# Last output columns taken token tile by token tile, three key splits placed ahead of the residual adds, nine constant products in the first gap, spreads as transposes

## The chip, the cores and the metric

The kernel runs on one core of a Trainium2 chip, in one launch. The metric is the device time of that launch in microseconds, the median of several runs. The time before is 1063.87 us, median of 3 runs (1063.2 to 1066.58).

The engines are named as in the profile: PE (TensorE, the products), DVE (VectorE), ACT (ScalarE), POOL (GpSimd), SP (SyncE, which issues most of the DMAs). PEld is the loading of a product's stationary operand.

## The reference, cut to what matters

Two layers of a streaming encoder over 512 tokens of width 1024, with a memory of 256 tokens. All values are 32-bit floats.

```python
for l in range(DEPTH):                       # 2
    h = rms_norm(x, norm_g[l])
    proj = h @ w_in[l]                       # pool, attention, indexer, memory query, gates
    y_pool = multi_scale_pool(...) * silu(pool_z)
    y_attn = dsa_attention(...) * silu(az)   # 8 heads, 128 selected keys a query
    mk, mv = split(rms_norm(mem, mem_norm_g[l]) @ w_mem_kv[l])
    y_mem = memory_attention(mq, mk, mv) * silu(mz)   # 4 heads of 128
    g = sigmoid(gates)                       # three gates a channel
    merged = g0 * (y_pool @ w_branch[l, 0]) + g1 * (y_attn @ w_branch[l, 1]) + g2 * (y_mem @ w_branch[l, 2])
    x = x + merged @ w_out[l]
return rms_norm(x, final_g)
```

`rms_norm(x, g)` is `x * rsqrt(mean(x * x) + EPS) * g` over the 1024 channels of a token.

## The kernel before, in words

**Products in three terms.** Nearly every operand is split into a high part (`whi`, `hh`, `memh`, `mgh`), a cast of it to the type fp32r, and a low part (`wlo`, `hl`, `meml`, `mgl`), the rest; a product is then hi x hi + hi x lo + lo x hi, three matmuls into one PSUM bank (`mm3`, `mm3v`). A weight chunk of 128 x 1024 is fetched by a DMA on SP's queue (`raw_chunk`, L165), cast by ACT (L173, `whi`) and subtracted by DVE, or by POOL where `eng=G` is given (L152 and L177, `wlo`). Raw chunks, `whi` and `wlo` have four buffers each, so a chunk's cast waits until PE has done with the chunk four before.

**Order.** The program's order is that of the source, which a scheduling layer then rearranges among instructions that are free to move; `tc.issue_after` and `behind_pe` pin a block behind a named instruction. Within an engine the order is then fixed. PSUM has eight banks by tag: `pj` 3, `at` 2, `tr` 2, `pv` 1.

**Start (layer 0).** 15 constant products of a 128 x 128 tile of ones, `busy`, run on PE first (L358 to L360). Then the memory's keys: 96 matmuls in four chunks. Then, behind them, `norm_cols` (L235): the squares of x, added up over the eight channel tiles by ACT (L229) and DVE (L232), are summed over the channels by products with a column of `ones`; `rstd_cols` turns the sums into the inverse root with a multiply-add on DVE (L215) and a power on POOL (L216). `spread` (L219) makes a 128 x 512 bank from the four columns of the result, each by a product of the column, broadcast to 128 x 128, with the identity. The memory's values stand in four groups of 12 matmuls (`mem_v`) between these steps: group, spread, group, the memory's column sums (of squares that POOL adds up, L417), group, the memory's spread, group. `norm_x` (L243) makes hf, hh and hl from x and the spread on DVE and ACT, and the index projection (`w_idx`, 24 matmuls into `tr`) reads them.

**Layer.** Projections, the indexer's scores, the selection in rounds on DVE, attention heads and branch projections follow. Then the output projection `out_half` (L311) for the two halves f of the output columns: for each of four chunks c of `w_out`, for each of four token tiles t, six matmuls into the tile's bank; after all of them four adds to the residual (L323, DVE), four squares with a sum (L324, ACT) and, in layer 0, the store of x for the next layer (L326, ACT's queue).

**Between the layers** (L938 to L964). The next layer's memory keys, four groups of 24 matmuls of 256 columns (`mem_k`), stand on PE after the output projection. The first and the second group's low parts were written for DVE and two others for POOL (`eng=G`), the latter behind the norm's power; the scheduling layer has moved groups so that the chunks are fetched in the order 0, 2, 3, 1, chunks 0 and 1 are split on DVE and chunks 2 and 3 on POOL, and PE runs chunk 0, then 2 and 1 interleaved, then 3. `rstd_of` (L329) makes the tokens' inverse root, `xr` the scaled x (L948 ACT, L949 DVE), `turn_x` (L336) turns it into `hh` and `hl` by PE transposes (L341), two channel tiles at a time, between the key groups and the first value groups.

**End (layer 1).** Half 0 is multiplied by the final gain on POOL (L933). After half 1, for each token tile: inverse root, `finish` (L346): two products by it on ACT and DVE (`o`) and a store each on ACT's and SP's queue.

## Time and profile before

| | us |
|---|---|
| median of 3 runs | 1063.87 |
| the profiled execution, its own time | 1065.19 |
| its span, first to last instruction | 1063.0 |
| what lies around the span | 2.19 |
| PE busy in the span | 1047.3 |
| DVE, ACT, POOL busy | 698.0, 474.1, 219.9 |
| mean granted clock of PE | 0.992 |

A row of a timeline has start, length, engine, source line, operation, out<-in, shapes and, in brackets, how long the engine had been idle before it and what ended that. A row of a list of waits has the waiting engine and line, what it waited for, total us, times and the longest. A row of a windows table has the stretch, its length, each engine's busy time with the number of instructions, then the granted clock, DMA share and GB/s; the tables below that were asked for PE alone have one busy column. A 32-bit product with a 128 x 128 moving operand that is not a transpose appears as two records. PE's lengths overlap, since products are pipelined, so their starts are compared.

### The profile page before, as it was taken

To read this page: it belongs to the slowest core of one execution; us is meant where nothing else is said; L and a number is where in the kernel's file an instruction comes from. 1 tells how busy PE (TensorE), PEld (TensorE's weight loads), DVE (VectorE), ACT (ScalarE), POOL (GpSimd) and SP (SyncE) were. 2 spreads that over 40 slices of the span, in tenths; PEclk is the share of its full clock that TensorE was granted. 3 is DMA by queue.
4 is the path that set the end of the run, shared out by engine and by line. 5 is a ranking of instruction groups with operands and counts; after the bars stand their busy time and mean duration, and the time that the engine had idled before them with its cause. 6 is when DMAs were issued, how large, how long until landed. Compare 5 with 4: busy or idle time off the path is not lost.

```text
span 1063.0 us, 13609 instructions
## 1 busy us (share of the span) xinstructions
PE 1047.3 (99%) x5024; PEld 883.4 (83%) x5024; DVE 698.0 (66%) x1273; ACT 474.1 (45%) x860; POOL 219.9 (21%) x293
## 2 busy tenths in 40 slices
PE   8999999999999999999999999999999999999996
PEld 8888888888888888888888888888888888888885
DVE  6757878787788855543374588787768887444342
ACT  7555554322555543432354545533236564333332
POOL 2301440002134410121060133100113333002131
PEclk9999999999999999999999999999999999999998
DMA  8432226323322322435354222222333331233332
GB/s 302 141 120 74 80 74 185 98 72 122 117 95 75 100 80 80 139 100 178 119 170 134 84 80 73 77 81 78 129 100 109 99 101 60 80 99 99 102 117 79
DMA packets 37986, 114.23 MB, mean 107 GB/s; under 512 B 4248, under 2 KB 6296, under 8 KB 37920
## 3 DMA queue, kind: packets, MB, share of 16 engines
q1 hardware_dynamic: 36048, 110.20, 31.5%
q10 hardware_dynamic: 1872, 3.17, 0.8%
q8 instruction: 39, 0.64, 0.2%
q14 instruction: 27, 0.22, 0.1%
HBM read 109.14 MB, written 6.84 MB: 109 GB/s over the span
## 4 chain that ended last, share of the span: by engine, by line
PE 92%; issue 4%; DMA 1%; ACT 1%; DVE 1%; POOL 0%; SPq 0%; ACTq 0%; POOLq 0%
PE pj L87 72%; PE at L87 8%; PE pv L87 6%; PE tr L87 2%; PE tr L607 2%; DMA wraw<-in_w_mk 1%; DMA x<-in_xT 1%; POOL sg L748 0%; DVE wlo L177 0%; ACT o L348 0%; ACT whi L173 0%; SPq L258 0%; PE at L341 0%; PE tr L341 0%; DVE sg L744 0%
## 5 line engine op out<-in xcount | busy, mean ns | idle before, releaser
L173 ACT CAST whi<-wraw 128x1024 fp32r<-128x1024 f32 (+1 forms) x174 | 182.0, 1046 | 375.1 <-PE pj L87 218.3
L87 PE MATMUL pj<-hh,whi 128*128 128x512 f32 (+1 forms) x848 | 330.2, 389 | 0.0
L87 PE MATMUL pj<-hh,wlo 128*128 128x512 f32 (+1 forms) x848 | 328.4, 387 | 0.0
L87 PE MATMUL pj<-hl,whi 128*128 128x512 f32 (+1 forms) x848 | 328.4, 387 | 0.0
L152 DVE TENSOR_TENSOR wlo<-wraw,whi 128x1024 fp32r<-128x1024 f32 x156 | 198.0, 1270 | 156.7 <-ACT whi L173 156.2
L87 PEld LDWEIGHTS pj<-hh,wlo 128*128 128x128 f32 x848 | 159.2, 188 | 32.1
L87 PEld LDWEIGHTS pj<-hl,whi 128*128 128x128 f32 x848 | 159.3, 188 | 30.6
L87 PEld LDWEIGHTS pj<-hh,whi 128*128 128x128 f32 x848 | 159.3, 188 | 30.6
L748 POOL TENSOR_TENSOR sg<-sg,sg 128x512 f32<-128x512 f32 x32 | 52.0, 1624 | 238.4 <-DVE sg L744 238.4
L87 PE MATMUL pj<-yh,whi 128*128 128x512 f32 x192 | 75.1, 391 | 0.0
L87 PE MATMUL pj<-yh,wlo 128*128 128x512 f32 x192 | 74.7, 389 | 0.0
L87 PE MATMUL pj<-yl,whi 128*128 128x512 f32 x192 | 74.7, 389 | 0.0
L792 POOL TENSOR_TENSOR p<-rel,acc 128x256 f32<-128x256 f32 (+2 forms) x48 | 61.3, 1298 | 0.5
L792 POOL TENSOR_TENSOR p<-rel,mask 128x128 f32<-128x128 f32 x16 | 7.4, 463 | 253.6 <-DMA rel<-bias_row 248.7
L744 DVE SCALAR_TENSOR_TENSOR sg<-sg,pj 128x512 f32<-128x512 f32 x48 | 32.9, 685 | 36.0 <-PE pj L87 35.9
L580 DVE MATCH_REPLACE8 acc<-m,acc 128x256 f32<-128x256 f32 (+2 forms) x96 | 51.4, 543 | 0.0
L579 DVE MAX8 m<-acc 128x8 f32<-128x256 f32 (+2 forms) x96 | 49.0, 548 | 0.1
L808 DVE CUSTOM_DVE_ANT_0 p<-at,p 128x128 f32<-128x128 f32 (+1 forms) x64 | 29.9, 490 | 27.6 <-PE at L87 23.8
L87 PEld LDWEIGHTS pj<-yh,wlo 128*128 128x128 f32 x192 | 36.0, 188 | 7.6
L87 PEld LDWEIGHTS pj<-yl,whi 128*128 128x128 f32 x192 | 36.1, 188 | 7.2
L87 PEld LDWEIGHTS pj<-yh,whi 128*128 128x128 f32 x192 | 36.0, 188 | 7.2
L813 DVE TENSOR_SCALAR p<-p,ast 128x128 f32<-128x128 f32 (+1 forms) x64 | 41.5, 678 | 0.3
(240 smaller groups left out, 1714.9 us busy)
## 6 DMA issues: line engine op xcount, KB each, us to landing
wraw<-in_w_tiled SPq DMA_DIRECT2D x112, 512.0 KB, 3.4
wraw<-in_w_br SPq DMA_DIRECT2D x24, 512.0 KB, 3.5
wraw<-in_w_out SPq DMA_DIRECT2D x16, 512.0 KB, 3.5
wraw<-in_w_mv SPq DMA_DIRECT2D x8, 512.0 KB, 4.6
wraw<-in_w_av SPq DMA_DIRECT2D x8, 512.0 KB, 3.8
rel<-bias_row SPq DMA_DIRECT2D x16, 256.0 KB, 3.8
wraw<-in_w_mk SPq DMA_DIRECT2D x7, 512.0 KB, 4.4
bias_row<-bias_one SPq DMA_DIRECT2D x8, 320.0 KB, 6.9
```

What stands on the lines that cost most here:

```text
L87: on_pe[:] = [T.matmul(*a, **kw)]
L152: eng.tensor_sub(out_lo, src, hi)
L173: A.copy(hi[:, :n], raw[:, :n])
L579: V.max(m8, a[:, :n])
L580: V.match_replace(out=a[:, :n], in_to_replace=m8, in_values=a[:, :n], imm_value=TAKEN)
L607: T.transpose(pt[:, i * P:(i + 1) * P], col_of(qb, kb), ident)
L744: last = V.scalar_tensor_tensor(s, s, 1.0, ps, op0=ALU.add, op1=ALU.mult)
L748: G.tensor_add(acc[j], acc[j], s)
L792: G.tensor_add(probs[h][:, Q_COL[qb]:Q_COL[qb] + n], rels[h][:, 512 - n:512], mb[:, :n])
L808: V.tensor_tensor_reduce(out=pq, in0=ps[:, :n], in1=pq, op0=ALU.add, op1=ALU.min, scale=-1.0, scalar=3e38, accum_out=st[:, 0, qb:qb + 1])
L813: V.tensor_scalar(pq, pq, st[:, 2, qb:qb + 1], None, op0=ALU.mult)
```

## The change

Five edits. The spread's products become transposes of the same broadcast columns (L223 after). Nine constant products are put between the memory's keys and the norm's column sums of layer 0. `out_half` becomes `out_part`, `out_add` and `out_banks`; half 0 of the last layer and both halves of layer 0 keep their order. In the last layer half 1 has its four chunks split first, and then each token tile runs through all four chunks, is added, squared, scaled and stored before the next. In layer 0 the next layer's first two key chunks are fetched and split between the last product of half 1 and its adds, the third behind the first key group, the fourth behind the second, all on DVE; and the transposes take their places after the third and fourth key group and after the first two value groups.

```diff
@@ -96,6 +96,7 @@
 
     N_S2 = 49
     N_BUSY = 15
+    N_GAP = 9
     SH1, PUMP1, PUMP2 = 0, 2, 9
     IQ_AT = (2, 3)
     MS = (2, 4, 5)
@@ -219,8 +220,7 @@
 
         pb = bank(tag)
         for b in range(nb):
-            matmul(pb[:, b * P:(b + 1) * P], r[:, b:b + 1].to_broadcast([P, P]), ident,
-                     start=True, stop=True)
+            on_pe[:] = [T.transpose(pb[:, b * P:(b + 1) * P], r[:, b:b + 1].to_broadcast([P, P]), ident)]
         return pb
 
     def norm_add(sums, k, xk, n=S, apart=KT - 1):
@@ -308,22 +308,24 @@
         return mv
 
 
-    def out_half(l, f, x, ssq):
-
-        bks = [bank("pv"), pj(), pj(), pj()] if f == 0 else [bank("at"), bank("at"), bank("tr"), bank("tr")]
-        for c in range(4):
-            hi, lo = chunk(w_out[l, f, c])
-            for t in range(NQ):
-                for a in range(2):
-                    k = 2 * c + a
-                    w = slice(a * 512, a * 512 + 512)
-                    tk = slice(t * P, t * P + P)
-                    mm3v(bks[t], mg_hi[k][:, tk], mg_lo[k][:, tk], hi[:, w], lo[:, w], k == 0, k == KT - 1)
-        for t in range(NQ):
-            V.tensor_add(x[t][f], x[t][f], bks[t])
-            A.activation(s2("sq"), x[t][f], AF.Square, scale=1.0 / 32, accum_out=ssq[:, f, t:t + 1])
-            if l + 1 < DEPTH:
-                nc.scalar.dma_start(x1[t * P:(t + 1) * P, f * 512:(f + 1) * 512], x[t][f])
+    def out_part(t, c, part, ps):
+
+        hi, lo = part
+        for a in range(2):
+            k = 2 * c + a
+            w = slice(a * 512, a * 512 + 512)
+            tk = slice(t * P, t * P + P)
+            mm3v(ps, mg_hi[k][:, tk], mg_lo[k][:, tk], hi[:, w], lo[:, w], k == 0, k == KT - 1)
+
+    def out_add(l, f, t, x, ssq, ps):
+
+        V.tensor_add(x[t][f], x[t][f], ps)
+        A.activation(s2("sq"), x[t][f], AF.Square, scale=1.0 / 32, accum_out=ssq[:, f, t:t + 1])
+        if l + 1 < DEPTH:
+            nc.scalar.dma_start(x1[t * P:(t + 1) * P, f * 512:(f + 1) * 512], x[t][f])
+
+    def out_banks(f):
+        return [bank("pv"), pj(), pj(), pj()] if f == 0 else [bank("at"), bank("at"), bank("tr"), bank("tr")]
 
     def rstd_of(ssq, ts):
 
@@ -405,6 +407,10 @@
                 matmul(o, w[:, c], r[k], start=k == 0 and h % 2 == 0 and n == 0, stop=k == KT - 1 and n == 2,
                        skip_group_check=True)
     with behind_pe():
+        ps = bank("at")
+        for i in range(N_GAP):
+            matmul(ps[:, :P], busy, busy, start=True, stop=True)
+    with behind_pe():
         r = norm_cols(sums)
     with tc.issue_after(on_dve[0].ins):
         parts_v[2:] = [split_chunk(raw, eng=V) for raw in parts_v[2:]]
@@ -926,40 +932,51 @@
             grow = s2("grow"), s2("grow")
             for f in range(2):
                 nc.sync.dma_start(grow[f], g_row[:, f * 512:(f + 1) * 512].to_broadcast([P, 512]))
-        for f in range(2):
-            out_half(l, f, x, ssq)
-            if last and f == 0:
+        for f in range(1 if last else 2):
+            bks = out_banks(f)
+            for c in range(4):
+                part = chunk(w_out[l, f, c])
                 for t in range(NQ):
+                    out_part(t, c, part, bks[t])
+            if f == 1:
+                ck = [chunk(w_mk[l + 1, h], eng=V) for h in range(2)]
+            for t in range(NQ):
+                out_add(l, f, t, x, ssq, bks[t])
+                if last:
                     G.tensor_mul(x[t][0], x[t][0], grow[0])
         if last:
+            parts_o = [chunk(w_out[l, 1, c]) for c in range(4)]
+            bks = out_banks(1)
             for t in range(NQ):
-                r = rstd_of(ssq, slice(t, t + 1))
-                finish(t, x, r, grow)
+                for c in range(4):
+                    out_part(t, c, parts_o[c], bks[t])
+                out_add(l, 1, t, x, ssq, bks[t])
+                finish(t, x, rstd_of(ssq, slice(t, t + 1)), grow)
         else:
             banks = []
-            mem_k(l + 1, 0, mh, ml, chunk(w_mk[l + 1, 0], eng=V), banks)
+            mem_k(l + 1, 0, mh, ml, ck[0], banks)
+            ck.append(chunk(w_mk[l + 1, 2], eng=V))
             r = rstd_of(ssq, slice(0, NQ))
-            with tc.issue_after(on_pool[0].ins):
-                c2, c3 = (chunk(w_mk[l + 1, h], eng=G) for h in (2, 3))
-            mem_k(l + 1, 1, mh, ml, chunk(w_mk[l + 1, 1], eng=V), banks)
+            mem_k(l + 1, 1, mh, ml, ck[1], banks)
+            ck.append(chunk(w_mk[l + 1, 3], eng=V))
+            mem_k(l + 1, 2, mh, ml, ck[2], banks)
             xr = []
             for t in range(NQ):
                 xr.append([s2("xr"), s2("xr")])
                 A.mul(xr[t][0], x[t][0], r[:, t:t + 1])
                 V.tensor_scalar(xr[t][1], x[t][1], r[:, t:t + 1], None, op0=ALU.mult)
             turn_x(l + 1, xr, (0, 4))
-            mem_k(l + 1, 2, mh, ml, c2, banks)
+            mem_k(l + 1, 3, mh, ml, ck[3], banks)
             turn_x(l + 1, xr, (1, 5))
-            mem_k(l + 1, 3, mh, ml, c3, banks)
-            turn_x(l + 1, xr, (2, 6))
             mkf = mem_k_norm(banks)
             pv = [pj(), bank("pv")]
             for c in range(4):
                 part = chunk(w_mv[l + 1, c], eng=G)
                 for b in range(2):
                     mem_v(l + 1, c, b, mh, ml, part, pv)
-                if c == 0:
-                    turn_x(l + 1, xr, (3, 7))
+                if c < 2:
+                    turn_x(l + 1, xr, (2 + c, 6 + c))
+                if c == 1:
                     mk = mem_k_end(mkf)
             mv = mem_v_end(pv)
```

The three places at which the instructions stand otherwise, as rows of one engine in program order. PE in layer 0, from the last matmul of the memory's keys (`pj` from `memh` and `wlo`) to the first value group; before:

```order
L87 MATMUL pj_309<-memh_244,wlo_240 128x256
L87 MATMUL tr_408<-ones,sq_278 128x1 x4
L87 MATMUL tr_408<-ones,sq_298 128x1 x4
L87 MATMUL pj_310<-whi_300,memh_196 128x512
L87 MATMUL pv_311<-whi_300,memh_196 128x512
```

After:

```order
L87 MATMUL pj_309<-memh_244,wlo_240 128x256
L87 MATMUL at_408<-busy 128x128 x9
L87 MATMUL tr_418<-ones,sq_278 128x1 x4
L87 MATMUL tr_418<-ones,sq_298 128x1 x4
L87 MATMUL pj_310<-whi_300,memh_196 128x512
L87 MATMUL pv_311<-whi_300,memh_196 128x512
```

A row of nine products of `busy` stands between the keys and the column sums.

DVE between the layers, from the split of the last `w_out` chunk on: `wlo` rows are splits of weight chunks, `x` rows the residual adds, `rs_v` the norm, `xr` the scaled x; before:

```order
L152 TENSOR_TENSOR wlo_4742<-wraw_4739,whi_4741 128x1024
L177 TENSOR_TENSOR wlo_4788<-wraw_4785,whi_4787 128x1024
L323 TENSOR_TENSOR x_4489<-x_4489,at_4645 128x512
L323 TENSOR_TENSOR x_4491<-x_4491,at_4646 128x512
L323 TENSOR_TENSOR x_4493<-x_4493,tr_4647 128x512
L323 TENSOR_TENSOR x_4495<-x_4495,tr_4648 128x512
L332 SCALAR_TENSOR_TENSOR rs_v_4816<-ssq_4504 128x4
L949 TENSOR_SCALAR xr_4863<-x_4489,rs_r_4817 128x512
L177 TENSOR_TENSOR wlo_4835<-wraw_4832,whi_4834 128x1024
L949 TENSOR_SCALAR xr_4867<-x_4491,rs_r_4817 128x512
L949 TENSOR_SCALAR xr_4871<-x_4493,rs_r_4817 128x512
L949 TENSOR_SCALAR xr_4875<-x_4495,rs_r_4817 128x512
```

After:

```order
L153 TENSOR_TENSOR wlo_4752<-wraw_4749,whi_4751 128x1024
L178 TENSOR_TENSOR wlo_4782<-wraw_4779,whi_4781 128x1024
L178 TENSOR_TENSOR wlo_4788<-wraw_4785,whi_4787 128x1024
L178 TENSOR_TENSOR wlo_4835<-wraw_4832,whi_4834 128x1024
L322 TENSOR_TENSOR x_4499<-x_4499,at_4655 128x512
L322 TENSOR_TENSOR x_4501<-x_4501,at_4656 128x512
L322 TENSOR_TENSOR x_4503<-x_4503,tr_4657 128x512
L322 TENSOR_TENSOR x_4505<-x_4505,tr_4658 128x512
L334 SCALAR_TENSOR_TENSOR rs_v_4838<-ssq_4514 128x4
L967 TENSOR_SCALAR xr_4898<-x_4499,rs_r_4839 128x512
L178 TENSOR_TENSOR wlo_4869<-wraw_4866,whi_4868 128x1024
L967 TENSOR_SCALAR xr_4902<-x_4501,rs_r_4839 128x512
```

Two more splits, of the second and third key chunk, stand ahead of the four adds; the row behind the first `xr` is the split of the key chunk that is fetched last (`w_mk` 1 before, 3 after). On POOL the two splits that stood right behind the norm's power are gone, and the first value chunk's split stands there.

ACT in the last layer, from the square of half 1's first token tile on: `sq` are squares, `o` the products by the inverse root, DMA the stores; before:

```order
L324 ACTIVATE sq_9220,ssq_8950<-x_8935 128x512
L324 ACTIVATE sq_9223,ssq_8950<-x_8937 128x512
L324 ACTIVATE sq_9226,ssq_8950<-x_8939 128x512
L324 ACTIVATE sq_9229,ssq_8950<-x_8941 128x512
L348 ACTIVATE o_9235<-x_8934,rs_r_9232 128x512
L348 ACTIVATE o_9245<-x_8936,rs_r_9242 128x512
L350 DMA out<-o_9235 128x512
L350 DMA out<-o_9245 128x512
L348 ACTIVATE o_9255<-x_8938,rs_r_9252 128x512
L348 ACTIVATE o_9265<-x_8940,rs_r_9262 128x512
L350 DMA out<-o_9255 128x512
L350 DMA out<-o_9265 128x512
```

After:

```order
L323 ACTIVATE sq_9158,ssq_8960<-x_8945 128x512
L350 ACTIVATE o_9164<-x_8944,rs_r_9161 128x512
L352 DMA out<-o_9164 128x512
L323 ACTIVATE sq_9195,ssq_8960<-x_8947 128x512
L350 ACTIVATE o_9201<-x_8946,rs_r_9198 128x512
L352 DMA out<-o_9201 128x512
L323 ACTIVATE sq_9232,ssq_8960<-x_8949 128x512
L350 ACTIVATE o_9238<-x_8948,rs_r_9235 128x512
L352 DMA out<-o_9238 128x512
L323 ACTIVATE sq_9269,ssq_8960<-x_8951 128x512
L350 ACTIVATE o_9275<-x_8950,rs_r_9272 128x512
L352 DMA out<-o_9275 128x512
```

Each tile's `o` and store now stand ahead of the next tile's square.

## The prediction

> **What bounds the kernel now.** I read the page first, then what PE waited for, then the clock in windows of 3.41 us, then the timelines of the three stages that the change touches.
>
> From the page: PE's busy time and the granted clock in 40 slices.
>
> ```profile
> PE 1047.3 (99%) x5024; PEld 883.4 (83%) x5024; DVE 698.0 (66%) x1273; ACT 474.1 (45%) x860; POOL 219.9 (21%) x293
> ...
> PEclk9999999999999999999999999999999999999998
> ```
>
> PE is busy for 99% of the span. A change that leaves the products alone can only win where PE stands, or runs slowly, or after its last product. Who made PE wait (total us, times, longest):
>
> ```profile
> PE tr L87 <- DVE sq L232: 2.7, 1, 2.7
> PE pj L87 <- POOL wlo L177: 2.0, 1, 2.0
> ...
> PE pj L87 <- DVE wlo L177: 0.3, 1, 0.3
> ```
>
> So there are two long waits: 2.7 us before the norm's column sums at the start, and 2.0 us between the layers. The clock around them (window, PE's busy time, PEclk in the column behind it):
>
> ```profile
> 18.45:21.86 3.41, 1.03 (x10) 1.00 0.91 363
> 21.86:25.27 3.41, 3.41 (x13) 0.50 0.35 106
> 25.27:28.69 3.42, 3.42 (x10) 0.50 0.86 283
> ...
> 533.86:537.27 3.41, 1.36 (x11) 1.00 0.01 2
> 537.27:540.68 3.41, 3.08 (x15) 0.50 0.63 184
> ```
>
> After each wait the granted clock is 0.50, for 6.83 us at the start and 3.41 us between the layers. The windows in which PE was busy for 1.03 and 1.36 us of 3.41 are those before the fall. A wait thus costs its own length and half of the slow time behind it.
>
> **The change, part by part.** *The start.* The first seven rows are PE's (the two without an operation are from the chain of waits), then DVE's and POOL's.
>
> ```profile
> 20.83 2.63 PE L87 MATMUL tr<-ones,sq 128*128 128x1 f32 x16 [2.67 <-DVE sq L232]
> ...
> 28.79 0.89 PE at L87 x8
> ...
> 115.64 0.87 PE tr L607 x8
> ...
> 32.26 0.95 PE L87 MATMUL tr<-ones,sq 128*128 128x1 f32 x8
> 33.06 0.49 PE L87 MATMUL pj<-whi,memh 128*128 128x512 f32 x1
> ...
> 35.93 0.60 PE L87 MATMUL at<-ident,mem_col 128*128 128x128 f32 x4
> ...
> 39.13 0.40 PE L87 MATMUL tr<-hh,whi 128*72 128x512 f32 x1
> ...
> 21.59 2.36 DVE L177 TENSOR_TENSOR wlo<-wraw,whi 128x1024 fp32r<-128x1024 f32 x2 [0.91 <-ACT whi L173]
> 23.87 0.15 DVE L215 TENSOR_SCALAR rs_v<-tr 128x4 f32<-128x4 f32 x1
> ...
> 29.72 2.06 DVE L249 SCALAR_TENSOR_TENSOR hf<-x,gains,at 128x512 f32<-128x512 f32 x3 [3.34 <-PE at L87]
> ...
> 41.71 0.69 DVE L251 TENSOR_TENSOR hl<-hf,hh 128x512 fp32r<-128x512 f32 x1
> ...
> 24.11 1.94 POOL L216 TENSOR_TENSOR rs_r<-rs_v,mhalf 128x4 f32<-128x4 f32 x1 [20.31 <-DVE rs_v L215]
> 26.02 4.21 POOL L417 TENSOR_TENSOR sq<-sq,sq 128x512 f32<-128x512 f32 x3
> ...
> 489.49 2.14 POOL L748 TENSOR_TENSOR sg<-sg,sg 128x512 f32<-128x512 f32 x1 [2.13 <-DVE sg L744]
> ```
>
> A product of 128x128 is two records, so the four of a spread took 0.89 us, 0.22 each, and a transpose 0.87/8 = 0.11. The nine products are worth 9 x 0.22 = 2.0 us and stand in a wait of 2.67: they cost nothing, and leave 0.7 of it idle; the column sums queued behind them wait for DVE until 20.83 as before, and the bank that they write is next wanted by the memory's spread. Spreads by transposes save 4 x 0.11 and 2 x 0.11, 0.65 us in all. Trainium skill, "TensorE: Matmul & The Clock Gate", Terms, calls transposes four times as fast for FP32; the rows here give twice, and by the page's factor the saving would be about 1.0.
>
> If the clock holds, the 16 sums take twice the eight's 33.06 - 32.26 = 0.80, and end at 22.4. A group of 12 value products takes 35.93 - 33.06 = 2.87 and ends at 25.3. Here something else is late: rs_v stands on DVE behind two splits until 23.87 whatever PE does, and POOL's power ends at 26.05. PE therefore waits 0.85 us, spreads until 26.6, and has the second group done at 29.5. The eight sums of the memory then wait for POOL's three adds. They end at 30.23, or, if the last of them runs at the 2.14 us which such an add took beside DVE instead of 1.40, at 31.0; I take 30.6, since only the last stands beside DVE's first `hl`. Sums to 31.4, a group to 34.3, the short spread to 34.5, a group to 37.3: the index projection starts at 37.3 and not 39.13, **1.8 us**. The norm follows: DVE's first `hf` moves from 29.72 to about 26.7, and its last `hl` (41.71) is wanted by the last of the 24 products only some 4.9 us after the projection's start. Ends: 2.2 with the adds undisturbed; 0.1 if the clock falls once more, below.
>
> *Between the layers.* ACT, DVE, POOL and PE:
>
> ```profile
> 526.08 1.05 ACT L173 CAST whi<-wraw 128x1024 fp32r<-128x1024 f32 x1 [4.39 <-PE tr L87]
> ...
> 527.39 0.69 DVE L323 TENSOR_TENSOR x<-x,at 128x512 f32<-128x512 f32 x1 [9.88 <-PE at L87]
> ...
> 530.11 0.69 DVE L323 TENSOR_TENSOR x<-x,tr 128x512 f32<-128x512 f32 x1 [0.67 <-PE tr L87]
> ...
> 534.25 2.57 DVE L949 TENSOR_SCALAR xr<-x,rs_r 128x512 f32<-128x512 f32 x1 [1.14 <-POOL rs_r L333]
> ...
> 540.07 3.40 DVE L949 TENSOR_SCALAR xr<-x,rs_r 128x512 f32<-128x512 f32 x3
> ...
> 534.18 8.20 POOL L177 TENSOR_TENSOR wlo<-wraw,whi 128x1024 fp32r<-128x1024 f32 x3
> ...
> 531.27 0.28 PE L87 MATMUL pj<-memh,whi 128*128 128x256 f32 x1
> ...
> 534.15 0.28 PE L87 MATMUL pj<-memh,whi 128*128 128x256 f32 x1
> ```
>
> Before, the key chunks fetched second and third have their `wlo` on POOL behind the norm's power, from 534.18, though the third's `whi` is cast by 527.13. Now DVE does both ahead of the residual adds. The third split (two took 2.36, so 1.2) runs from 527.2 to 528.4, so the first add, queued behind it, moves from 527.39 to 528.4 and the second comes close behind; the third waited for PE's bank until 530.11 and stays there. ACT's squares and stores of the first two tiles follow their adds; from the third tile on nothing moves, and so `rs_v` does not. The four DMAs of the mk chunks keep their places on SP.
>
> PE then has three key groups of 2.88 us (534.15 - 531.27) in a row, until 539.9, and by then `xr` must be there. DVE starts it at 534.25. The 2.57 us there lay beside POOL's split; POOL now has none until the first value chunk's `whi`, which ACT casts only after two of its `xr`. With 0.7 for the first, as an add takes, 1.2 for the last key split and at worst the 3.40 for the other three, DVE ends at 539.5. That leaves 0.4 us. What goes is 2.0 + 0.3 of waiting and half of the 3.08 us at clock 0.50, 1.5: **3.9 us**. Ends: 2.3, if in other executions the clock did not fall there; 4.4, if the interleaved transposes cost something too.
>
> *The end.* PE (the first row from the chain of waits), DVE, ACT, POOL, the landing of the output's stores, and the last window:
>
> ```profile
> 1031.93 2.72 PE at L87 x12
> ...
> 1053.30 0.39 PE L87 MATMUL tr<-whi,mgl 128*128 128x512 f32 x1
> ...
> 1033.10 2.05 DVE L152 TENSOR_TENSOR wlo<-wraw,whi 128x1024 fp32r<-128x1024 f32 x1 [0.45 <-ACT whi L173]
> ...
> 1053.73 0.69 DVE L323 TENSOR_TENSOR x<-x,tr 128x512 f32<-128x512 f32 x1 [0.60 <-PE tr L87]
> ...
> 1054.98 0.19 ACT L324 ACTIVATION_READ_ACCUMULATOR sq<-x 128x1 f32 x1
> ...
> 1051.85 0.57 POOL L333 TENSOR_TENSOR rs_r<-rs_v,mhalf 128x1 f32<-128x1 f32 x1 [15.55 <-DVE rs_v L332]
> ...
> DMA to landing us min/median/max: 2.1/3.4/3.7
> ...
> 1061.70:1063.00 1.30, 0.00 (x0) 0.00 (x0) 0.00 (x0) 0.00 (x0) 0.00 (x0) 0.50 0.00 0
> ```
>
> After PE's last product (1053.69) the span goes on for 9.31 us: four tiles end one after another, and their eight stores queue. Now a tile ends with its 24 products, every 5.4 us (12 take 2.72), and only the last is left. Its square is read at 1055.17, `rs_v` takes 0.2 and the power 0.1 + 0.57, `o` 0.7 like an `hf`, so the stores go out at 1056.9; 2.1 to land, as the emptiest took, and 1.3 as before: 1060.3, **2.7 us**. Ends: 1.1, with a landing of 3.7; 3.1, if the last 1.3 shrinks too. Each store's issue on ACT now stands ahead of the next tile's square, which comes 5.4 us later. PE's count is the same. Its one new need is the fourth chunk after 18 products and not after 72: wanted at 1031.93 + 4.1 = 1036.0, split at 1035.15, as before; a cover of 0.85 us, in which the last three of the old half's adds and POOL's products by the final gain also lie.
>
> **The sum.** 1.8 + 3.9 + 2.7 = 8.4 us off the profiled execution's 1065.19 (its span of 1063.0 and 2.19 around it). That execution is 1.32 above the median of the runs, 1063.87; I take the same 8.4 off the median: 1055.5.
>
> **Rivals.** *The clock falls at the start all the same.* For: the nine products and the sums fill the window 18.45 to 21.86 with 1.65 us of wide products, not far above the 1.36 that was too little; and new waits of 0.85 and 1.1 us come at 25.3 and 29.5, the second followed by one-column sums, so that the window from 28.69 to 32.10 holds about 1.5 us of wide products. Against: 1.36 us was of a window with 2.05 in one piece idle. Half of 3.41 us is lost: 8.4 - 1.7 = 6.7, 1057.2.
>
> *Short waits do not cool the clock.* If in most executions the clock kept up through the two waits, they cost only their length: 0.65 + 2.3 + 2.7 = 5.65, 1058.2. Against it, both waits of this execution, 2.67 and 2.05, were followed by 0.50. Trainium skill, "TensorE: Matmul & The Clock Gate", Part 1 and Why this matters for your kernels, speaks for this one: the clock falls after at least one idle window of about 3.4 us, and only gaps of over some 3 us are to be avoided. On the shorter gaps the trace disagrees; on the free-running windows that the page describes it agrees, with 6.83 and 3.41 us at half clock.
>
> *The norm's `xr` is late.* If DVE runs as slowly as before (last `xr` at 543.4), the transposes wait 3.5 us at 539.9 and the clock falls behind that, 1.7: the 3.9 become -1.3, the sum 3.2, 1060.7, no change that can be told. Against: POOL's splits, beside which that was, now start later.
>
> *Slower: the third key split blocks DVE.* It stands ahead of all four residual adds. Were it L later than 528.4, norm, `xr` and transposes would be L later, with 0.4 of cover, and 1.7 for the clock: from L = 7.1 on all 8.4 are gone, and at L = 10.3 the kernel is 3.2 slower, 1067.1. Against: its `whi` waits only for PE's slot (526.08), as before.
>
> **How the numbers follow.** Chances: forecast 0.50, clock at the start 0.36, short waits 0.08, late `xr` 0.04, blocked DVE 0.02. A measurement of this kernel can tell about 0.3%, 3.2 us: the first three are faster (0.94), the fourth is the same, the last slower. The range goes from 1053.2 (2.2 + 4.4 + 3.1 = 9.7, and 1 for the runs' scatter) to 1058.8 (the third case and 0.6 of scatter).
>
> **What would show it.** Right: PEclk 1.00 from 18 to 40 us and from 530 to 562; PE's list of waits without POOL's `wlo`; the index projection at 37.3; some 26 us from the first key product to the second layer's index projection; 6.6 us after the last product. Wrong: a window at 0.50 behind 21.9 or 32; a wait of PE on `xr`; stores of the last tile landing in over 3 us. If the end gains less than 1 us or the boundary less than 2, the forecast fails.

## The result, and the profile after

The changed kernel takes 1056.14 us (median of 6 runs, 1055.76 to 1057.74), beside 1063.45 us for the kernel before (median of 6 runs, 1063.14 to 1066.58). The ratio is 0.9929, with a 95% interval of 0.9916 to 0.9942: 7.3 us less. The profiled execution took 1056.66 us, its span 1055.0, where before it was 1065.19 and 1063.0; between these two executions lie 8.5 us. The ratios below leave out two runs of the kernel before (1502.3 and 1762.38 us) and one of memory_norm_early (1501.17 us), in which the mean granted clock was 0.56 to 0.65.

The page of the changed kernel, PE's busy time and the granted clock, and below it what made PE wait (total us, times, longest):

```profile
PE 1044.9 (99%) x5036; PEld 881.5 (84%) x5036; DVE 694.6 (66%) x1275; ACT 474.6 (45%) x860; POOL 214.8 (20%) x291
...
PEclk9999999999999999999999999999999999999999
```

```profile
PE tr L87 <- DVE sq L232: 1.9, 1, 1.9
PE at L87 <- DVE busy L359: 1.0, 1, 1.0
```

Both waits between the layers are gone, POOL's and DVE's `wlo`. Of the long waits only the one ahead of the norm's column sums is left, 1.9 us of it behind the nine products. The clock in the windows that were shown of before, and in windows laid where the clock changes in this execution (length, PE busy, PEclk in the column behind):

```profile
18.45:21.86 3.41, 1.55 (x15) 1.00 0.95 377
21.86:25.27 3.41, 3.41 (x22) 0.90 0.24 75
25.27:28.69 3.42, 3.42 (x13) 0.60 0.83 275
533.86:537.27 3.41, 3.41 (x31) 1.00 0.46 145
537.27:540.68 3.41, 3.41 (x32) 1.00 0.38 102
...
17.77:21.19 3.42, 1.86 (x17) 1.00 1.04 410
21.19:24.60 3.41, 3.11 (x22) 1.00 0.21 75
24.60:28.01 3.41, 3.41 (x11) 0.50 0.81 253
```

Between the layers the clock stays at 1.00. At the start it fell after all, for one window of 3.41 us from 24.60 on and not for two: a window at 0.50 behind 21.9 is what the prediction named as a sign of being wrong. The stages can be read from PE's rows: column sums, first spread, the memory's sums and the index projection at the start, then the first key product of layer 1, its index projection, and the last product.

```profile
21.49 1.92 PE L87 MATMUL tr<-ones,sq 128*128 128x1 f32 x16 [1.86 <-DVE sq L232]
...
27.40 0.90 PE L223 MATMUL at<-ident,rs_r 128*128 128x128 f32 x4
...
30.97 1.05 PE L87 MATMUL tr<-ones,sq 128*128 128x1 f32 x8
...
37.67 0.40 PE L87 MATMUL tr<-hh,whi 128*72 128x512 f32 x1
...
529.81 0.28 PE L87 MATMUL pj<-memh,whi 128*128 128x256 f32 x1
...
555.75 0.40 PE L87 MATMUL tr<-hh,whi 128*72 128x512 f32 x1
...
1047.65 0.39 PE L87 MATMUL tr<-whi,mgl 128*128 128x512 f32 x1
```

The second index projection of before, which 30.16 rests on:

```profile
561.43 0.40 PE L87 MATMUL tr<-hh,whi 128*72 128x512 f32 x1
```

Against the rows of before: the index projection 39.13 - 37.67 = 1.46 earlier; from the first key product to the second index projection 555.75 - 529.81 = 25.94 and not 30.16, 4.22 less; from the last product's end (1048.04) to the end of the span 6.96 and not 9.31, 2.35 less. The long stretches between these points are as long as before: 492.14 and 492.14 us from index projection to key products, 492.29 and 492.26 to the last product. 1.46 + 4.22 + 2.35 = 8.03, the 8.0 us between the spans.

What lies around the span became shorter too: 2.10 to 2.23 us in all runs of the kernel before that list a span, 1.65 to 1.79 in those of the changed one, 0.44 less.

### The profile page after: what moved, and what is told of

It reads as the page before. It is cut to its first block, busy times and chain, and to the rows that moved or that the text cites. A ratio compares the mean times of both kernels' runs of the same rounds, so it can differ in the third digit from the quotient of the medians.

```text
span 1055.0 us, 13635 instructions
## 1 busy us (share of the span) xinstructions
PE 1044.9 (99%) x5036; PEld 881.5 (84%) x5036; DVE 694.6 (66%) x1275; ACT 474.6 (45%) x860; POOL 214.8 (20%) x291
## 4 chain that ended last, share of the span: by engine, by line
PE 96%; DMA 1%; issue 1%; ACT 1%; SPq 0%; DVE 0%; POOLq 0%; POOL 0%; ACTq 0%
PE pj L87 75%; PE at L87 9%; PE pv L87 7%; PE tr L87 3%; PE tr L613 2%; DMA x<-in_xT 1%; DMA wraw<-in_w_mk 1%; ACT whi L174 0%; PE tr L343 0%; PE at L343 0%; SPq L258 0%; ACT kh L782 0%; ACT kh L781 0%; SPq L377 0%; PE at L223 0%
```

## The experiments

Eleven kernels, compared with the kernel before on the same chip in groups: four (before: median 1064.89), four (1064.3) and three (1063.4). This table is read from the profiles: the idle time ahead of the column sums of x, how many windows of 3.41 us at clock 0.50 followed, the time from these sums to the index projection, and the two other stages; then the median of the runs.

| kernel | idle | slow windows | sums to index projection | first key product to 2nd index projection | after the last product | median us |
|---|---|---|---|---|---|---|
| before | 2.67 | 2 | 18.30 | 30.16 | 9.31 | 1063.45 |
| only_boundary | 1.62 | 0 | 16.49 | 25.94 | 9.42 | 1058.63 |
| only_last | 1.83 | 1 | 16.72 | 30.14 | 6.81 | 1060.61 |
| only_gap | 0.36 | 1 | 16.73 | 30.13 | 9.33 | 1063.18 |
| fill_boundary | 3.22 | 2 | 18.30 | 33.29 | 9.43 | 1067.96 |
| changed | 1.86 | 1 | 16.18 | 25.94 | 6.96 | 1056.14 |
| no_gap | 2.08 | 1 | 16.23 | 25.94 | 6.86 | 1055.68 |
| splits_on_pool | 0 | 0 | 16.49 | 25.93 | 6.83 | 1057.19 |
| spreads_as_products | 0.20 | 0 | 16.48 | 25.93 | 6.89 | 1055.90 |
| memory_norm_early | 1.44 | 1 | 15.99 | 25.94 | 7.13 | 1058.01 |
| changed_again | 0.99 | 1 | 16.22 | 25.93 | 6.86 | 1055.81 |
| no_start_edits | 1.57 | 1 | 16.72 | 25.94 | 6.95 | 1056.08 |
| early_rs | 0 | 2 (later) | 19.72 | 25.94 | 6.87 | 1056.17 |

**only_boundary**: the kernel before with the new order between the layers.

```diff
+            if f == 1 and not last:
+                ck = [chunk(w_mk[l + 1, h], eng=V) for h in range(2)]
             for t in range(NQ):
                 out_add(l, f, t, x, ssq, bks[t])
...
-            mem_k(l + 1, 0, mh, ml, chunk(w_mk[l + 1, 0], eng=V), banks)
+            mem_k(l + 1, 0, mh, ml, ck[0], banks)
+            ck.append(chunk(w_mk[l + 1, 2], eng=V))
...
```

> The kernel before with the edit between the layers alone (key splits ahead of the residual adds, transposes in their new places; spreads, gap and last columns as before). Theory, waits and clock both count: PE's waits of 2.05 and 0.33 us and half of the 3.08 us at clock 0.50 go, so from the first key product of layer 1 to its index projection it takes 25.9 us and not 30.16, and the median is 4.2 below 1063.45, at 1059.2. Rival, the clock mostly held through a wait of 2.05 us when no profile is taken: only the 2.3 us of waiting go, 1061.1. Rival, the gain belongs to the changes at the start: no change here.

1058.63 us, ratio 0.9947 (0.9934 to 0.9961). The stage took 25.94 us, as the first theory said. The median fell by 6.3, more than 4.2, since this group's runs of before fall in two kinds (below); from lowest run to lowest run it is 1063.05 - 1058.43 = 4.6, which is the 4.2 and the 0.44 around the span (1.68 to 1.74 here).

**only_last**: the kernel before with the last output columns token tile by token tile.

```diff
+            parts_o = [chunk(w_out[l, 1, c]) for c in range(4)]
+            bks = out_banks(1)
             for t in range(NQ):
-                r = rstd_of(ssq, slice(t, t + 1))
-                finish(t, x, r, grow)
+                for c in range(4):
+                    out_part(t, c, parts_o[c], bks[t])
+                out_add(l, 1, t, x, ssq, bks[t])
+                finish(t, x, rstd_of(ssq, slice(t, t + 1)), grow)
```

> The kernel before with the last output columns token tile by token tile alone. Theory: after PE's last product 6.96 us are left and not 9.31, PE waits nowhere in the last 40 us, and the median falls by 2.35 to 1061.1. Rival, the early need of all four chunks costs a wait on DVE's split of up to 1 us: 1062. Rival, the stores of one tile land as late as those of four did: less than 1 us, about 1063.

1060.61 us, ratio 0.9966 (0.9953 to 0.9978); lowest to lowest 2.6. The end took 6.81 us, and PE did not wait in the last stage. What this kernel's waits show lies elsewhere, between the layers, where its code is that of before:

```profile
PE pj L87 <- POOL wlo L178: 2.0, 1, 2.0
PE tr L87 <- DVE sq L233: 1.8, 1, 1.8
PE pj L87 <- DVE wlo L178: 1.5, 1, 1.5
```

Here POOL's wait is again 2.0 us, but the wait for DVE's `wlo` is 1.5 and not 0.3. The windows around the two waits, laid at whole multiples of 3.41 us from where the clock changes at the start of this execution:

```profile
530.91:534.32 3.41, 1.75 (x15) 1.00 0.21 79
534.32:537.73 3.41, 2.14 (x16) 1.00 0.50 154
```

The wait of 2.05 us lay across two windows, and the clock did not fall. And yet the stage took 30.14 us, as in before, where the clock fell for a window.

**only_gap**: the kernel before with the nine products.

```diff
     with behind_pe():
+        ps = bank("at")
+        for i in range(N_GAP):
+            matmul(ps[:, :P], busy, busy, start=True, stop=True)
+    with behind_pe():
         r = norm_cols(sums)
```

> The kernel before with the nine constant products in the first gap alone. Theory: they end before the column sums can start and so delay nothing, and they keep the clock at 1.00 for one window more; the index projection comes 16.8 us behind the column sums and not 18.3, and the median falls by 1.5 to 1062.0. Rival, the clock falls one window later all the same and costs as much: 1063.4, no change. Rival, POOL's adds of the memory's squares set the time of the memory's sums, whatever the clock: 0.7 to 1.0 us less, 1062.6.

1063.18 us in 11 runs beside 1064.89 in 15, ratio 0.9989 (0.998 to 0.9998). The profile has the index projection 16.73 us behind the sums, as the first theory said, though the clock did fall for one window. The lowest runs lie together, 1062.84 and 1063.05: the products change the slower runs of before, not its faster ones. Between the layers, windows of this profile, laid where the clock changes:

```profile
531.91:535.33 3.42, 1.37 (x12) 1.00 0.13 48
535.33:538.74 3.41, 3.41 (x16) 0.50 0.47 159
```

The same wait of 2.05 us lay in one window here, PE was busy for 1.37 of 3.41 us, and the clock fell. PE then had no wait for DVE's `wlo`, and the stage took 30.13.

**fill_boundary**: the kernel before with nine constant products in the wait between the layers.

```diff
             mem_k(l + 1, 0, mh, ml, chunk(w_mk[l + 1, 0], eng=V), banks)
+            with behind_pe():
+                ps = bank("at")
+                for i in range(N_GAP):
+                    matmul(ps[:, :P], busy, busy, start=True, stop=True)
             r = rstd_of(ssq, slice(0, NQ))
```

> The kernel before with nine constant products put in its wait between the layers, behind the first key group; the wait for POOL's split stays as long as it was, and the first transposes stand in a row behind the second key group. Theory, a wait of 2 us cools the clock: it stays at 1.00, and from the first key product to the index projection it takes 30.16 - 1.5 = 28.6 us, the median 1.5 lower, 1061.9. Rival, the wait costs its length alone: 30.2 us and no change, 1063.45.

1067.96 us, ratio 1.0034 (1.0021 to 1.0047): slower, and for another reason than either theory. The pinned products also changed the order behind them, so that the key group that DVE splits last now came second:

```profile
PE pj L87 <- DVE wlo L178: 3.6, 1, 3.6
```

It does not answer the question about the clock; only_last and only_gap do.

**no_gap**: the changed kernel without the nine products.

```diff
     with behind_pe():
-        ps = bank("at")
-        for i in range(N_GAP):
-            matmul(ps[:, :P], busy, busy, start=True, stop=True)
-    with behind_pe():
         r = norm_cols(sums)
```

> The changed kernel without the nine constant products, all else the same. The earlier runs showed column sums to index projection in 18.30 us where the clock was at 0.50 for two windows behind the first wait, 16.73 with one and 16.49 with none. Theory, only a second slow window costs anything, and the products prevent it: some runs come out 1.5 us slower and others as before, so that the lowest run is within 0.3 of the changed kernel's 1055.76 and the median lies 0.3 to 1.5 above 1056.14. Rival, as the prediction summed: every run loses half a slow window at least, so the lowest run is above 1057 and the median near 1057.6. Rival, the products do nothing: 1056.1.

1055.68 us, ratio 0.9919 (0.9904 to 0.9935): not slower than the changed kernel's 0.9929. PE's start, with a wait of 2.08 us and one slow window:

```profile
20.89 1.92 PE L87 MATMUL tr<-ones,sq 128*128 128x1 f32 x16 [2.08 <-DVE sq L232]
...
30.38 1.05 PE L87 MATMUL tr<-ones,sq 128*128 128x1 f32 x8
...
37.12 0.40 PE L87 MATMUL tr<-hh,whi 128*72 128x512 f32 x1
```

16.23 us from sums to index projection, as with the products. Five of the six runs lie between 1055.31 and 1056.04; the lowest is below the changed kernel's, and so is the median. The products do not earn anything here.

**splits_on_pool**: the changed kernel with two key splits on POOL again.

```diff
-                ck = [chunk(w_mk[l + 1, h], eng=V) for h in range(2)]
+                ck = [chunk(w_mk[l + 1, h], eng=(V, G)[h]) for h in range(2)]
...
-            ck.append(chunk(w_mk[l + 1, 2], eng=V))
+            ck.append(chunk(w_mk[l + 1, 2], eng=G))
```

> The changed kernel with the second and third key splits back on POOL, but still ahead of the residual adds and of the norm's power. Theory, what mattered was their place behind the norm's power, which also put them beside DVE's scaled x: POOL does them by about 528, first key product to index projection stays at 25.9 us and the time at 1056.1, within 0.5. Rival, POOL is too slow for them wherever they stand: PE waits for POOL's split, 27 us or more, 1057.5 and above. What lies around the span, 1.72 us with the new boundary and 2.16 with the old one, stays at 1.72 if it goes by the place and returns to 2.16 if it goes by the engine.

1057.19 us, ratio 0.9931 (0.9917 to 0.9946). POOL's rows:

```profile
519.75 2.39 POOL L178 TENSOR_TENSOR wlo<-wraw,whi 128x1024 fp32r<-128x1024 f32 x1 [30.15 <-ACT whi L174]
525.19 2.40 POOL L178 TENSOR_TENSOR wlo<-wraw,whi 128x1024 fp32r<-128x1024 f32 x1 [3.05 <-ACT whi L174]
531.17 1.03 POOL L335 TENSOR_TENSOR rs_r<-rs_v,mhalf 128x4 f32<-128x4 f32 x1 [3.58 <-DVE rs_v L334]
```

Both splits are done by 527.6, and the stage took 25.93 us: for the stage in this profile the place ahead of the norm is what counts, not the engine. The theory's time was missed: the median is 1.1 above it. 0.2 to 0.3 of that lie around the span (1.86 to 2.07, between the old and the new value); the rest is not explained. The profiled run is one of the two fast ones (1056.29); the other four lie between 1056.97 and 1058.36, and no profile shows what is longer in them.

**spreads_as_products**: the changed kernel with the spreads of before.

```diff
-            on_pe[:] = [T.transpose(pb[:, b * P:(b + 1) * P], r[:, b:b + 1].to_broadcast([P, P]), ident)]
+            matmul(pb[:, b * P:(b + 1) * P], r[:, b:b + 1].to_broadcast([P, P]), ident,
+                     start=True, stop=True)
```

> The changed kernel with the two spreads as products again. Theory, both lie on PE's path where it does not wait behind the spread for POOL's adds: in the profile the first spread takes 0.89 us and not 0.48, column sums to index projection 0.2 to 0.65 us longer, 1056.3 to 1056.8. Rival, POOL's adds of the memory's squares cover them: no change, 1056.1.

1055.9 us, ratio 0.9922 (0.9908 to 0.9937): no change that can be told. In its profile the clock held, and PE waited for POOL and DVE:

```profile
PE at L87 <- POOL rs_r L217: 0.5, 1, 0.5
PE tr L87 <- POOL sq L424: 0.3, 1, 0.3
PE tr L87 <- DVE sq L233: 0.2, 1, 0.2
```

The stage took 16.48 us, where splits_on_pool, with transposes and the clock held too, took 16.49: in both, PE waited for POOL's adds ahead of the memory's sums (0.3 us here, 1.1 there), so what transposes save only made that wait longer.

**changed_again** and **no_start_edits**: the changed kernel, and beside it the same with both start edits undone: the diffs of no_gap and of spreads_as_products in one kernel.

> The changed kernel once more, beside the kernel without the start edits on the same chip. Theory: 1056.1 within 0.7, sums to index projection 16.2 to 16.5 us, no run with two slow windows at the start.

> The changed kernel with both start edits undone: no products in the first gap, spreads as products. What is left are the new order between the layers and the last columns token tile by token tile. Theory: these two carry 4.2 + 2.35 in the span and 0.44 around it; the start edits take away the case of two slow windows, which cost the kernel before 1.6 us in more than half of its runs, so the median lies between that of the changed kernel and 1.6 above it, and the lowest run within 0.4 of the changed kernel's lowest. Rival, as the prediction summed: 1.8 us slower in every run, 1057.9. Rival, the start edits are worth nothing on their own: the same median within 0.4.

1055.81 us, ratio 0.9925 (0.9913 to 0.9937), and 1056.08 us, ratio 0.9927 (0.9915 to 0.9939). The second rival holds: the start edits bring nothing that can be told in the kernel with the other edits. The first theory's bounds hold this median too, but not its reason: no run of no_start_edits has the mean clock of one with two slow windows (0.996 and above; the runs of early_rs with two have 0.995). In the two profiles, each with one slow window, the stage differs by 16.72 - 16.22 = 0.5 us. That goes with the transposes (no_gap, which has them without the products, took 16.23), but does not show in the median.

**memory_norm_early**: a further rearrangement of the start.

```diff
+    sq = []
+    for k in range(4):
+        sq.append(s2("sq", shape=(P, 2, M)))
+        A.activation(sq[-1], mem0[k], AF.Square)
+        if k > 0:
+            G.tensor_add(sq[0], sq[0], sq[-1])
     x = [s2("x") for _ in range(KT)]
...
     with behind_pe():
+        col = bank("tr")
+        for a in range(2):
+            square_sums(col, sq[0][:, a, :], 2, a == 0, a == 1)
+        with tc.issue_after(added.ins):
+            rstd_cols(col, 2, mem_col)
+    with behind_pe():
         r = norm_cols(sums)
...
```

> The changed kernel with the start rearranged further: ACT squares the memory and POOL adds it up while the keys are multiplied, the memory's column sums stand in the first gap behind the nine constant products, four more constant products stand behind the column sums of x, and the second value split goes behind the norm's multiply-add on DVE. Theory, in the changed kernel the start is bound by the chain from DVE's rs_v over POOL's power and three adds (until 30.9) to the memory's sums: without them PE runs through, column sums to index projection 14.7 us and not 16.2, and the median is 1.4 lower, 1054.7. Rival, DVE's norm is the next bound: its last hl comes too late for the index projection and PE waits there, 0.5 lower at most. Rival, ACT's squares of the memory delay the squares of x, and the sums come later by as much as is won: 1056.1 or above.

1058.01 us (median of five runs), ratio 0.9944 (0.9928 to 0.9961), 1.9 above the changed kernel. The sums came later, as the last rival has it, but only in part through ACT. POOL's adds ran beside DVE's splits and adds (DVE's rows first):

```profile
11.04 1.29 DVE L385 TENSOR_TENSOR wlo<-wraw,whi 128x512 fp32r<-128x512 f32 x2
...
13.93 3.10 DVE L385 TENSOR_TENSOR wlo<-wraw,whi 128x512 fp32r<-128x512 f32 x2 [0.80 <-ACT whi L384]
...
19.63 3.08 DVE L233 TENSOR_TENSOR sq<-sq,sq 128x512 f32<-128x512 f32 x4
...
13.47 1.30 POOL L392 TENSOR_TENSOR sq<-sq,sq 128x512 f32<-128x512 f32 x1 [9.67 <-ACT sq L390]
15.10 3.09 POOL L392 TENSOR_TENSOR sq<-sq,sq 128x512 f32<-128x512 f32 x2 [0.33 <-ACT sq L390]
```

The last two half splits had to wait 0.80 us for ACT, whose cast stood behind two squares of the memory; they then took 3.10 us, where the two before them took 1.29 with POOL idle. The adds of x ended at 22.71 and not at 21.34 as in the changed kernel, so the column sums came at 22.77.

**early_rs**: the changed kernel with the second value split behind the norm's `rs_v`.

```diff
-        parts_v[:2] = [split_chunk(raw, eng=V) for raw in parts_v[:2]]
+        parts_v[:1] = [split_chunk(raw, eng=V) for raw in parts_v[:1]]
...
-        parts_v[2:] = [split_chunk(raw, eng=V) for raw in parts_v[2:]]
+        parts_v[1:] = [split_chunk(raw, eng=V) for raw in parts_v[1:]]
```

> The changed kernel with the second value split placed behind the norm's rs_v on DVE. Theory: where the clock holds, PE waits 0.5 us on POOL's power and 0.3 to 1.1 on POOL's adds, both queued behind rs_v, which stood behind a split of 1.2 us; rs_v comes 1.1 us earlier, these waits go, column sums to index projection 15.4 to 15.9 us and the median 0.5 to 1.0 lower, 1055.4. Rival, the second value group then waits for its split, which ends as late as the first did: no gain, 1056.1. Rival, in runs with a slow window PE has no wait there, so nothing is won.

1056.17 us, ratio 0.9932 (0.9918 to 0.9946): nothing won, and two of six runs at 1059.5. The profile is of one of these. `rs_v` came at 22.77 as meant, but POOL's adds wait for ACT's squares, and PE, now earlier, waited longer for them:

```profile
20.81 1.92 PE L87 MATMUL tr<-ones,sq 128*128 128x1 f32 x16
...
30.63 1.77 PE L87 MATMUL tr<-ones,sq 128*128 128x1 f32 x8 [1.83 <-POOL sq L423]
```

```profile
27.33:30.74 3.41, 1.58 (x8) 1.00 0.80 292
30.74:34.15 3.41, 3.41 (x13) 0.50 0.23 59
34.15:37.57 3.42, 3.42 (x10) 0.50 0.28 110
```

The wait of 1.83 us lay in one window, the next began with one-column sums, and the clock fell for two windows: 19.72 us from the sums to the index projection.

## Why the prediction was right, and which step of it failed

The direction, the range and the two larger terms held. 1055.5 was forecast and 1056.14 measured: 7.3 us less instead of 8.4. That the two times lie so near is in part luck: the 1.8 us of the start, which the median does not show, were in part made up for by 0.44 us that no term had, by 0.3 more between the layers, and by a kernel before whose median is 1063.45 over six runs and not 1063.87.

**Between the layers**, 3.9 us were forecast and 4.22 measured in the span. The order of events came as written: the third split ran ahead of the first add (525.70 to 526.93), the add moved behind it, and the third add still waited for PE's bank. The `xr` were ready sooner than I allowed:

```profile
525.70 1.23 DVE L178 TENSOR_TENSOR wlo<-wraw,whi 128x1024 fp32r<-128x1024 f32 x1 [4.21 <-ACT whi L174]
526.85 1.28 DVE L322 TENSOR_TENSOR x<-x,at 128x512 f32<-128x512 f32 x2
528.65 0.69 DVE L322 TENSOR_TENSOR x<-x,tr 128x512 f32<-128x512 f32 x1 [0.53 <-PE tr L87]
...
532.79 0.49 DVE L967 TENSOR_SCALAR xr<-x,rs_r 128x512 f32<-128x512 f32 x1 [1.14 <-POOL rs_r L335]
533.19 1.22 DVE L178 TENSOR_TENSOR wlo<-wraw,whi 128x1024 fp32r<-128x1024 f32 x1
534.33 1.27 DVE L967 TENSOR_SCALAR xr<-x,rs_r 128x512 f32<-128x512 f32 x3
```

One `xr` takes 0.49 us where POOL is idle; beside POOL's split it took 2.57, and the key split 3.40 and not 1.22. DVE was done with them at 535.60, ahead of the first transposes at 538.45 by 2.9 us and not by 0.4 (ACT's last `xr` ended at 536.30), and the rival of the late `xr` is out. The Trainium skill, "SBUF — State Buffer", section "SBUF: two separate sides", says that DVE and POOL take a shared pair of ports in turns, each for a whole instruction; the longer instructions (2.57 and 3.40 us) agree with it.

But the working inside this term was wrong. I added the waits (2.3) and half of the slow window (1.5) as two things that go. In only_last the clock did not fall, and the second wait grew from 0.33 to 1.46 instead; in only_gap it fell and there was no second wait; before and these two took 30.13 to 30.16. PE met DVE's last key split either way; in before it is this row, and PE's next product follows at 540.20:

```profile
536.75 3.40 DVE L177 TENSOR_TENSOR wlo<-wraw,whi 128x1024 fp32r<-128x1024 f32 x1
```

The split ended at 540.15 in before, at 538.26 in only_last and at 538.72 in only_gap, and PE's next product came 0.05 to 0.06 us later in all three, whether PE had run slowly until then or had waited. So the slow window had no price of its own; what set the stage was the chain from the adds over the norm, an `xr` and the last split, the last two stretched by POOL. The sum came out near since wait and slow time together are most of what PE lost against that chain, however they share it: in only_last, at clock 1.00, PE stood idle for 3.51 us of the stage. The other 0.69 of its 4.20 us over the changed kernel is longer busy time (26.63 us and not 25.94 for as many instructions). There the scheduling layer had put transposes singly between the key products, a cost that the forecast had only in its upper end of 4.4; no run tests it alone. The 0.44 around the span was in no term. It came with the new order between the layers (only_boundary has it, only_last not); by what way stays open.

**The end**: 2.7 forecast, 2.35 measured. The step that was mis-sized is the landing. The stores went out 3.1 us after the last product, where 3.2 were written (the terms named there add up to 3.05), then took at least 2.6 and not 2.1, and 1.2 followed, where 1.3 were summed. SP's last issue, and the landing of the output's stores:

```profile
1051.16 0.33 SPq L353 DMA_DIRECT2D out<-o  x1
```

```profile
DMA to landing us min/median/max: 2.6/2.7/2.9
```

**The start** is where the prediction failed, at the step "I take the same 8.4 off the median". Its 1.8 us were made against the profiled execution, which had two slow windows and stood 1.3 above the median. Between the two profiled executions it is nearly right: the sums came 0.66 later and the index projection 1.46 earlier, 2.1 of the stage. (The wait ahead of the sums ends with a DMA: ACT's last two squares of x stood idle for `x<-in_xT` until 19.33 in before and 19.99 in the changed kernel, the same 0.66 later; over the profiles here the sums start anywhere from 20.12 to 21.59, memory_norm_early aside.) The working for a clock that holds was right, 37.3 - 20.83 = 16.47 us, where the two profiles of the changed kernel's variants in which it held have 16.48 and 16.49. In the median it is worth nothing that can be told (changed_again against no_start_edits: 1055.81 and 1056.08). The profiles say why. With no slow window and with one the stage takes 16.0 to 16.7 us, with two 18.3 and more. So the first slow window is free: where the clock holds, PE waits for POOL's power and adds (0.5 and 0.3 us in spreads_as_products, 0.5 and 1.1 in splits_on_pool), and where it falls for one window PE meets them just in time, in the changed kernel at 30.97:

```profile
26.69 4.23 POOL L423 TENSOR_TENSOR sq<-sq,sq 128x512 f32<-128x512 f32 x3
```

They end at 30.92. Only a second window costs, 1.6 to 1.8 us, and the runs of before fit that by and large: 17 of 34 have a mean clock of at most 0.993, with a median of 1065.06, and the other 17 a median of 1063.33. (The count leaves out one run of 1065.67 us at a mean clock of 0.943. It is rough: the mean clock also counts the window between the layers and the tail, and three of the other 17 take 1065.0 to 1065.73, so something else lengthens runs too.)

Of the rivals, "the clock falls at the start all the same" had the event right: a window that held the sums took the clock down, from 24.60 on. Its price of 1.7 us was wrong, for the reason above. "Short waits do not cool the clock" is wrong as a rule, since waits of 0.36 to 3.62 us were followed by slow windows, and right in part: a wait of 2.05 did not cool it in only_last. What separates the two in these profiles is how much of one window of 3.41 us PE is busy with wide products, the windows laid where the clock changes. In all 13 profiles, around the two stages, the windows at clock 1.00 with at most 1.51 us of wide products were followed by 0.50, and those with 1.57 or more by 1.00. The two nearest to that border are of no_start_edits and of spreads_as_products:

```profile
20.23:23.65 3.42, 3.29 (x23) 1.00 0.53 186
```

```profile
18.35:21.76 3.41, 3.21 (x30) 1.00 0.94 374
```

The first counts 3.29 us as busy, but 1.78 of them are one-column sums; 1.51 are left, and the clock fell to 0.50. The second counts less, 3.21, with 1.64 of sums; 1.57 are left, and the clock stayed at 1.00. In the changed kernel's window from 21.19 to 24.60 it is 3.11 less 1.78, 1.33, and the clock fell. The Trainium skill, "TensorE: Matmul & The Clock Gate", Part 1, has the clock fall after an idle window of some 3.4 us; in the runs here a window a little over half idle is enough, if the one-column sums are counted as idle. That the windows run free, as the same section says, agrees with the same wait cooling in one execution and not in another.

What adds up in the median is therefore 4.22 between the layers, 0.44 around the span and 2.35 at the end, 7.0 of the 7.3 us; the rest is within the scatter of the runs.

When a second slow window follows can be read off: in the three profiles with two (before, fill_boundary, early_rs) the first slow window itself held 1.6 to 2.1 us of one-column sums, in the seven with one at most 0.5. It takes a fall that comes before the sums are through. Open stays why that is so frequent in the kernel before (17 of 34 runs, going by the mean clock) and absent, by the same measure (0.996 and above), in the eleven runs of no_gap and no_start_edits, whose start has the same wait without the products. The wait was somewhat shorter in their profiles (2.08 and 1.57 us, 2.67 in before), since the first keys ended later, but nothing that was tried sets that. In only_boundary and only_last, whose start is that of before, only one run of five each stands 1.2 us or more above the others (1060.2 and 1062.39).

## What to carry to other kernels

Before slow clock is priced at half its length, look for what PE meets behind it: if another engine's chain ends later anyway, the slow time only replaces a wait. A profile is one execution; where it stands above the median, find out what it has that the others lack, and do not take that off the median. Work for POOL and DVE that stands side by side should be moved apart in time, as the key splits were here; the engine matters less than the place.

## What the runs showed of the hardware

- A 128 x 512 scaling on DVE took 0.4 to 0.5 us with POOL idle and 2.57 beside a POOL split; a 128 x 1024 split 1.22 and 3.40.
- One-column products keep PE busy in the profile, but not its clock: a window with 3.29 us of 3.41 busy, 1.78 of it in such products, was followed by 0.50 (no_start_edits), one with 1.86 us of wide products alone by 1.00 (changed).
- What lies around the span (1.7 or 2.2 us) depends on the program: 0.44 us went with an edit in its middle, and half of it came back with two splits on POOL.
